# Head pairs of q, k and all of v in products of 512 weight columns, a pad in the pooling pool, and phasors as an outer product

## The chip, the cores and the metric

The kernel runs on one core of a Trainium2 chip. The metric is the device time of one execution in microseconds (us), taken as the median of repeated runs. The profile and the trace are of one execution, recorded by the hardware profiler; that execution has a time of its own, beside the span that the trace covers. The engines are PE (TensorE, matrix products; PEld is its loading of the stationary operand), DVE (VectorE), ACT (ScalarE), POOL (GpSimd), and SP (SyncE), which here only issues DMAs.

## The reference

One block of an encoder: a normalised input of 1024 tokens by 1024 channels is multiplied by a wide weight matrix, the columns go to four mixers, and the gated mixers' outputs are merged.

```python
hn = rms_norm(x, norm_scale[i])
z = hn @ w_in[i]                       # 1024 x 1024 by 1024 x 9216
a_x, a_g, q, k, v, b_g, c_x, c_g, d_x, d_g, merge = jnp.split(z, split_points, axis=-1)
y_a = rglru_mixer(a_x, ...) * jax.nn.silu(a_g)                  # gated linear recurrence
y_b = neighbourhood_attention(q, k, v, ...) * jax.nn.silu(b_g)  # 8 heads of 64 channels
y_c = s5_mixer(c_x, ...) * jax.nn.silu(c_g)                     # diagonal complex recurrence
y_d = pool_mixer(d_x, ...) * jax.nn.silu(d_g)                   # windows of 2, 4, 8, 16
ys = jnp.stack([y_a, y_b, y_c, y_d], axis=2)
gates = jax.nn.sigmoid(merge.reshape(bsz, s, 4, 1024))
merged = jnp.sum(jnp.einsum('bsnw,nwd->bsnd', ys, w_branch[i]) * gates, axis=2)
x = x + merged @ w_out[i]
x = x + jax.nn.sigmoid(x @ ple_gate[i]) * (p[i] @ ple_proj[i])
```

q, k and v are 512 channels each, columns 1024 to 2560 of `w_in`. In the s5 mixer every one of 32 groups has 64 states and two directions, which makes 128 complex decay factors per group; the kernel works on blocks of 8 tokens and needs the powers of a phasor per state for 128 block positions.

## The kernel before

**Products.** Every fp32 operand is split into a high and a low part (`split`, L85: ACT copies the high part, DVE subtracts), and a product is three matmuls (`mm3`, L89): high by high (L94), low by high (L95 in a row of the trace) and high by low (L96). A row names the moving operand, then the stationary one: `ps_z<-wh,hnH` streams weight columns past stationary normalised tokens, `ps_z<-hnH,wh` streams tokens past stationary weights.

**q, k, v.** These are wanted with tokens on the partitions, so the stationary operand is a block of 128 tokens of `hnH` or `hnL` and 256 weight columns move past it (`tok_gen`, L210: 8 token blocks x 8 blocks of the sum x 3 matmuls). `at_z(rd)` (L453) makes 128 columns of q and 128 of k, which is one head pair, for round `rd` of 4; `at_w` (L447) loads them. v is made in two such products (`tok_product`, L418). So six products of 192 matmuls each, of 128x256.

**Fill.** All other columns of z run through `z_gen` (L158): 128 weight columns stationary, 512 tokens moving, 24 matmuls a piece. The generator `fill` (L355) yields these pieces in the order s5 input, gates of branch 2, merge gates 1, and so on; the attention takes one piece of `side` or `fill` for each of its units (`attention`, L400), and the stages s5, glu and lru take as many as `drive` (L189) gives them, to keep PE at work beside DVE. What is left runs before `pool`.

**Buffers.** Raw weights `wr`, their parts `wh` and `wl` (three of each), and two buffers `gz` of 128x1024, used by results that go to DRAM (`su`, `gz`), are shared by all of this. `s5_u` (L892) sends the s5 input to DRAM as `ud` from `gz` buffers, four stores in all. The stages' own buffers come from pools that are opened one after the other in the same memory: `pool` (L697) opens its own (`up`, `pa`, `pm`, ...) where those of `lru` lay, and the merge's (`mp`) are opened ahead of it.

**s5.** `s5_params` (L755) makes tables once. Each of four batches (`s5_batch`, L916) makes its phasors `E` from line 998 on by seven doublings: in each the part done is multiplied by a power `Pm[m]`, on 8, 16, ... 512 elements a partition.

**Order.** The order of the instructions on each engine is set when the kernel is built: a scheduler plays them against a model of the engines, and every engine then runs its list in order. The text of the program, the costs that pieces yield and the pools' buffers decide it together.

Of the kernel before, what the change touches and what calls it, by code (L numbers as in the profile page):

```python
# [9 lines left out]
F32 = mybir.dt.float32  # L10
# [10 lines left out]
W = 512  # L21
# [10 lines left out]
class Kern:  # L32
    def __init__(self, tc, es, ins, out):
# [15 lines left out]
        self.yd = [self.dp.tile([W, S], F32, name=f"yd{n}") for n in range(4)]  # L49

# [149 lines left out]

    def w_tok_halves(self, raw):

        out = []
        for kh in range(2):
            H, L = self.whl([128, 4, 256])
            self.split(H, L, raw[:, 4 * kh:4 * kh + 4, :])
            out += [(H[:, k, :], L[:, k, :]) for k in range(4)]
        return out

    def tok_gen(self, aH, aL, raw, consume):  # L210

        hl = self.w_tok_halves(raw)
        for t in range(8):
            ps = self.ps("z")[:, :256]
            c = slice(t * 128, t * 128 + 128)
            self.mm3(ps, [(aH[k][:, c], aL[k][:, c], hl[k][0], hl[k][1]) for k in range(8)])
            consume(t, ps)
            yield 2.6, 0.0

    def tok_product(self, aH, aL, raw, consume):  # L220
        for _ in self.tok_gen(aH, aL, raw, consume):
            pass
# [151 lines left out]
    def start(self):  # L374
        with self.tc.tile_pool(name="st", bufs=1, reuse_waits="tile") as st:
# [12 lines left out]
            raw0 = self.at_w(0)  # L388
# [5 lines left out]
            self.zq0 = next(self.z0)  # L394
# [5 lines left out]
    def attention(self, ap, fill):  # L400
        nc = self.nc
        vd = self.dp.tile([S, W], F32, name="vd")
        z = [self.at_z(rd) if rd else self.z0 for rd in range(4)]
        zq = [self.zq0]
# [4 lines left out]
        for _ in z[0]:  # L409
            pass  # L410
        prep = self.at_prep(ap, 0, zq[0])
# [3 lines left out]
        for vb in range(2):  # L415
            raw = self.wload_in(2048 + 256 * vb)

            def put_v(t, ps, vb=vb):  # L418
                v = ap.tile([128, 256], F32, tag="vtok", name="vtok", bufs=2)
                self.copy_a(v, ps)  # L420
                nc.sync.dma_start(vd[t * 128:t * 128 + 128, vb * 256:vb * 256 + 256], v)
            self.tok_product(self.hnH, self.hnL, raw, put_v)
            if vb == 0:
                self.lru_consts()
        zq.append(next(z[1]))
        for _ in z[1]:
            pass
        for rd in range(4):
            nxt, prep = None, iter(())
            if rd < 3:  # L430
                prep = self.at_prep(ap, rd + 1, zq[rd + 1])
                nxt = next(prep)
                next(prep)
            side = fill
            if rd < 2:
                side = z[rd + 2]
                zq.append(next(side))
            for u, _ in enumerate(self.at_units(ap, rd, qk, bias, vd)):
                next(side, None)
                if u == 3:  # L440
                    next(prep, None)
            if rd < 2:
                for _ in side:
                    pass
            qk = nxt

    def at_w(self, rd):  # L447
        win = self.i["w_in"]
        return self.wload([(lambda r_, s=s: r_[:, :, s * 128:s * 128 + 128],
                            win[:, c0:c0 + 128].rearrange("(k p) n -> p k n", p=128))  # L450
                           for s, c0 in ((0, 1024 + 128 * rd), (1, 1536 + 128 * rd))])

    def at_z(self, rd, raw=None):  # L453

        raw = raw or self.at_w(rd)
        zqk = self.zp.tile([128, 8, 256], F32, tag="zqk", name="zqk", bufs=2)
        ss = self.zp.tile([128, 32], F32, tag="ss", name="ss", bufs=2)
        yield zqk, ss

        def put(t, ps):  # L460
            self.copy_a(zqk[:, t, :], ps)
# [956 lines left out]
```

## Time and profile before

| | us |
|---|---|
| median of 3 runs | 1363.79 (1362.86 to 1364.15) |
| the profiled execution, its own time | 1363.28 |
| its span in the trace | 1361.5 |
| PE busy | 1346.4 (99%) |
| PEld busy | 1142.4 (84%) |
| DVE busy | 918.7 (67%) |
| ACT busy | 565.0 (41%) |

A busy share says how long at least one instruction of the engine was in work. PE's matmuls overlap, so the duration of one (its latency) is longer than the distance from its start to the next one's start; how many fit into a stretch is read from the distances. A wait is listed with the engine whose result ended it.

### The profile page before, as it was taken

Reading aid. Unit: us, or ns where it says so; the run is one execution under the profiler, and the core shown is the slowest. Engines: PE = TensorE matmul, PEld = TensorE weight load, DVE = VectorE, ACT = ScalarE, POOL = GpSimd, SP = SyncE. Lnnn points to the kernel's source line nnn. Section 1 sums busy time; section 2 is a strip of 40 time slices with the busy share of each in tenths; the row PEclk is TensorE's granted clock in tenths of the full one; section 3 lists DMA queues with packets and bytes.
Section 4 is the critical chain, followed back from the end, with each engine's and each line's share of the span. In section 5 each row is a group of like instructions: output and inputs, shape, how many; then the busy total and the mean of one; then the engine's idle time right before and its main releaser. Section 6 shows DMA issues by size and latency. Waiting matters only on the chain.

```text
span 1361.5 us, 19175 instructions
## 1 busy us (share of the span) xinstructions
PE 1346.4 (99%) x7360; PEld 1142.4 (84%) x7360; DVE 918.7 (67%) x1666; ACT 565.0 (41%) x882; POOL 20.6 (2%) x81
## 2 busy tenths in 40 slices
PE   7999999999999999999999999999999999999998
PEld 6999998888888888788888888888888888888887
DVE  6551676455279797988758477266456667797797
ACT  6542676587532222222225545536321211145553
POOL 2200000000000000000000000000000000000000
PEclk9999999999999999999999999999999999999999
DMA  9452134433244233333344242241834747533435
GB/s 327 130 144 68 51 85 123 132 97 121 85 116 124 81 100 107 110 97 94 128 131 179 70 143 77 97 147 71 298 127 151 248 158 251 212 109 118 130 124 186
DMA packets 141198, 181.98 MB, mean 134 GB/s; under 512 B 29216, under 2 KB 101160, under 8 KB 141106
## 3 DMA queue, kind: packets, MB, share of 16 engines
q1 hardware_dynamic: 140754, 180.72, 40.9%
q8 instruction: 58, 0.95, 0.3%
q14 instruction: 34, 0.28, 0.1%
q0 software_dynamic: 352, 0.03, 0.0%
HBM read 127.05 MB, written 54.03 MB: 133 GB/s over the span
## 4 chain that ended last, share of the span: by engine, by line
PE 92%; DVE 5%; issue 1%; ACT 1%; DMA 0%; SPq 0%; DVEq 0%
PE ps_z L94 15%; PE ps_z L95 15%; PE ps_z L96 15%; PE ps_t L95 4%; PE ps_t L96 4%; PE ps_t L94 4%; PE ps_t L99 3%; PE ps_o L94 3%; PE ps_z L1335 3%; PE ps_t L1335 3%; PE ps_s L1335 3%; PE ps_o L96 3%; PE ps_o L95 3%; PE ps_o L1335 3%; PE ps_s L94 3%; PE ps_s L96 3%
## 5 line engine op out<-in xcount | busy, mean ns | idle before, releaser
L94 PE MATMUL ps_z<-hnH,wh 128*128 128x512 f32 x744 | 293.2, 394 | 2.0 <-DVE bgt L60 2.0
L95 PE MATMUL ps_z<-hnL,wh 128*128 128x512 f32 x744 | 292.0, 392 | 0.0
L96 PE MATMUL ps_z<-hnH,wl 128*128 128x512 f32 x744 | 291.8, 392 | 0.0
L94 PEld LDWEIGHTS ps_z<-hnH,wh 128*128 128x128 f32 x744 | 139.8, 188 | 30.9 <-DVE bgt L60 2.4
L96 PEld LDWEIGHTS ps_z<-hnH,wl 128*128 128x128 f32 x744 | 139.8, 188 | 28.4 <-issue 0.4
L95 PEld LDWEIGHTS ps_z<-hnL,wh 128*128 128x128 f32 x744 | 139.8, 188 | 27.9 <-issue 0.4
L66 DVE TENSOR_TENSOR wl<-wr,wh 128x1024 fp32r<-128x1024 f32 x72 | 88.0, 1222 | 100.8 <-ACT wh L82 100.7
L82 ACT ACTIVATE wh<-wr 128x1024 fp32r<-128x1024 f32 x72 | 76.1, 1059 | 147.5 <-PE ps_z L95 81.2
L94 PE MATMUL ps_z<-wh,hnH 128*128 128x256 f32 x384 | 108.3, 285 | 0.5 <-ACT zqk L82 0.5
L96 PE MATMUL ps_z<-wh,hnL 128*128 128x256 f32 x384 | 108.5, 287 | 0.0
L95 PE MATMUL ps_z<-wl,hnH 128*128 128x256 f32 x384 | 108.1, 283 | 0.0
L95 PE MATMUL ps_t<-hnL,wh 128*128 128x512 f32 x216 | 84.2, 390 | 0.0
L94 PE MATMUL ps_t<-hnH,wh 128*128 128x512 f32 x216 | 84.1, 389 | 0.0
L96 PE MATMUL ps_t<-hnH,wl 128*128 128x512 f32 x216 | 84.0, 389 | 0.0
L94 PEld LDWEIGHTS ps_z<-wh,hnH 128*128 128x128 f32 x384 | 73.3, 192 | 1.2 <-ACT zqk L82 1.2
L95 PEld LDWEIGHTS ps_z<-wl,hnH 128*128 128x128 f32 x384 | 73.5, 192 | 0.0
L96 PEld LDWEIGHTS ps_z<-wh,hnL 128*128 128x128 f32 x384 | 72.9, 192 | 0.0
L551 DVE CUSTOM_DVE_ANT_0 sc<-ps_s,bias 128x384 f32<-128x384 f32 x64 | 34.2, 554 | 27.2 <-PE ps_s L545 14.6
L94 PE MATMUL ps_o<-my,wh 128*128 128x512 f32 x128 | 49.9, 390 | 0.4 <-DVE pm L69 0.4
L78 ACT ACTIVATE gz<-ps_z 128x512 f32<-128x512 f32 x45 | 26.6, 592 | 56.9 <-issue 35.1
L94 PE MATMUL ps_s<-my,wh 128*128 128x512 f32 x128 | 49.8, 389 | 0.0
L96 PE MATMUL ps_s<-my,wl 128*128 128x512 f32 x128 | 49.8, 389 | 0.0
(411 smaller groups left out, 2707.2 us busy)
## 6 DMA issues: line engine op xcount, KB each, us to landing
wr<-in_w_in_dram SPq DMA_DIRECT2D x32, 1024.0 KB, 5.2
gd<-gz SPq DMA_DIRECT2D x32, 512.0 KB, 2.8
mgt<-gd SPq DMA_DIRECT2D x32, 512.0 KB, 4.1
sg<-bgt SPq DMA_DIRECT2D x16, 512.0 KB, 3.2
my<-yd SPq DMA_DIRECT2D x16, 512.0 KB, 4.3
mbr<-in_w_branch_dram SPq DMA_DIRECT2D x8, 1024.0 KB, 6.3
bias<-E SPq DMA_DIRECT2D x128, 48.0 KB, 2.0
xt<-in_x_dram SPq DMA_DIRECT2D x8, 512.0 KB, 10.0
```

The source lines that it names most:

```text
L66: self.nc.vector.tensor_tensor(out, a, b, ALU.subtract)
L78: self.nc.scalar.activation(out, a, f, **kw)
L82: return self.nc.scalar.activation(out, a, AF.Copy)
L94: mm(ps, aH, bH, start=(k == 0), stop=False)
L95: mm(ps, aH, bL, start=False, stop=False)
L96: mm(ps, aL, bH, start=False, stop=(k == n - 1))
L99: self.nc.tensor.transpose(ps, src, self.ident[:k, :k])
L551: nc.vector.tensor_tensor_reduce(sc, pss[h], bias[g][h][:, VIDX[j], :], 1.0, -3e38, ALU.add, ALU.max, mx)
L1335: self.nc.tensor.matmul(acc[g][:, n2], a[:, k, c], b[:, k, n2], start=begin and a is aH and b is bH, stop=end and a is aL, skip_group_chec ...
```

## The change

It has three parts.

1. **Wide products.** `at_z(pr)` makes q and k of two head pairs in one product: 256 columns of q and 256 of k, 512 moving columns. `qk_load` loads them in four DMAs, and `qkv_tiles` splits the weights in four chunks, of which three lie in `wh`/`wl` buffers and the fourth in the two `gz` buffers. v is one product of 512 columns. In rounds 0 and 1 of the attention the side work is now the first half of the s5 input (4 pieces), then the second wide product, then `fill`; the other half of the s5 input opens `fill`.
2. **A pad in `pool`.** One tile of 3600 floats a partition is taken and never used, which puts the following buffers of the pool at higher addresses, behind the memory of `lru`.
3. **Phasors.** `s5_params` makes two small tables for all 32 groups, `Ef` with the first 16 powers and `Eh` with every 16th of 128; a batch multiplies them as an outer product, three operations of 128x1024 for each of the real and imaginary parts.

```diff
...
             self.nc.vector.tensor_copy(self.gT, pt[:, 0:8])
             ple = self.ple(st, *ab, *hl)
             next(ple)
-            raw0 = self.at_w(0)
+            raw0 = self.qk_load(0)
             self.rel_bias()
             self.norm(st, 0, x0)
             for _ in ple:
                 pass
             self.z0 = self.at_z(0, raw0)
-            self.zq0 = next(self.z0)
+            self.zq = next(self.z0)
             for _ in range(4):
                 next(self.z0)
             self.norm(st, 1, x1)
     def attention(self, ap, fill):
         nc = self.nc
         vd = self.dp.tile([S, W], F32, name="vd")
-        z = [self.at_z(rd) if rd else self.z0 for rd in range(4)]
-        zq = [self.zq0]
+        zq = self.zq
         bias = [[ap.tile([128, 3, 384], F32, name=f"bias{g}{h}") for h in range(2)] for g in range(2)]
         for b in bias[0] + bias[1]:
             nc.gpsimd.memset(b, NEG)
         self.at_buffers(ap)
-        for _ in z[0]:
+        for _ in self.z0:
             pass
+        raw_v = self.wide_load("w_in", 2048)
         prep = self.at_prep(ap, 0, zq[0])
         qk = next(prep)
         for _ in prep:
             pass
-        for vb in range(2):
-            raw = self.wload_in(2048 + 256 * vb)
-
-            def put_v(t, ps, vb=vb):
-                v = ap.tile([128, 256], F32, tag="vtok", name="vtok", bufs=2)
-                self.copy_a(v, ps)
-                nc.sync.dma_start(vd[t * 128:t * 128 + 128, vb * 256:vb * 256 + 256], v)
-            self.tok_product(self.hnH, self.hnL, raw, put_v)
-            if vb == 0:
+        for t, ps in self.qkv_tiles(raw_v):
+            v = ap.tile([128, 512], F32, tag="vtok", name="vtok")
+            self.copy_a(v, ps)
+            nc.sync.dma_start(vd[t * 128:t * 128 + 128, :], v)
+            if t == 3:
                 self.lru_consts()
-        zq.append(next(z[1]))
-        for _ in z[1]:
-            pass
+        side = self.z_gen([self.s5_u(0)])
         for rd in range(4):
-            nxt, prep = None, iter(())
-            if rd < 3:
+            prep = iter(())
+            if rd != 1 and rd < 3:
                 prep = self.at_prep(ap, rd + 1, zq[rd + 1])
                 nxt = next(prep)
                 next(prep)
-            side = fill
-            if rd < 2:
-                side = z[rd + 2]
-                zq.append(next(side))
             for u, _ in enumerate(self.at_units(ap, rd, qk, bias, vd)):
                 next(side, None)
+                if rd == 0 and u == 1:
+                    raw1 = self.qk_load(1)
                 if u == 3:
                     next(prep, None)
-            if rd < 2:
-                for _ in side:
-                    pass
+                    if rd == 0:
+                        side = self.at_z(1, raw1)
+                        zq = zq + next(side)
+                    if rd == 1:
+                        side = fill
+                        prep = self.at_prep(ap, 2, zq[2])
+                        nxt = next(prep)
+                if rd == 1 and u in (3, 4):
+                    next(prep, None)
             qk = nxt
 
...
+    def qk_load(self, pr):
+
+        out = []
+        for kh in range(2):
+            r = self.wp.tile([128, 4, 512], F32, tag="wr", name="wr")
+            for s in range(2):
+                c0 = 1024 + 512 * s + 256 * pr
+                self.nc.sync.dma_start(r[:, :, s * 256:s * 256 + 256],
+                                       self.i["w_in"][kh * 512:kh * 512 + 512, c0:c0 + 256]
+                                       .rearrange("(k p) n -> p k n", p=128))
+            out.append(r)
+        return out
+
+    def qkv_tiles(self, raws):
+
+        hl = []
+        for q in range(4):
+            if q < 3:
+                H, L = self.whl([128, 2, 512])
+            else:
+                H, L = (self.gzp.tile([128, 2, 512], F32R, tag="gz", name="w" + c) for c in "hl")
+            self.split(H, L, raws[q // 2][:, q % 2 * 2:q % 2 * 2 + 2, :])
+            hl += [(H[:, k, :], L[:, k, :]) for k in range(2)]
+        for t in range(8):
+            ps = self.ps("z")
+            c = slice(t * 128, t * 128 + 128)
+            self.mm3(ps, [(self.hnH[k][:, c], self.hnL[k][:, c]) + hl[k] for k in range(8)])
+            yield t, ps
+
+    def at_z(self, pr, raws):
+
+        out = [(self.zp.tile([128, 8, 256], F32, tag="zqk", name="zqk", bufs=2),
+                self.zp.tile([128, 32], F32, tag="ss", name="ss", bufs=2)) for _ in range(2)]
+        yield out
+        for t, ps in self.qkv_tiles(raws):
+            for r, (zqk, ss) in enumerate(out):
+                self.copy_a(zqk[:, t, :].rearrange("p (s n) -> p s n", s=2),
+                            ps.rearrange("p (s r n) -> p r s n", s=2, r=2)[:, r])
+                sq = self.zp.tile([128, 4, 64], F32, tag="sq", name="sq", bufs=2)
+                self.act(sq, zqk[:, t, :].rearrange("p (h c) -> p h c", c=64), AF.Square)
+                self.nc.vector.tensor_reduce(ss[:, t * 4:t * 4 + 4], sq, AX.X, ALU.add)
+            yield 5.2, 0.0
 
...
     def pool(self, pp):
         nc, i = self.nc, self.i
         ef = pp.tile([128, 4, 16], F32, name="ef")
+        pp.tile([128, 3600], F32, name="pad")
...
             self.cmul(sp, Pr[:, m + 1, :], Pi[:, m + 1, :], Pr[:, m, :], Pi[:, m, :], Pr[:, m, :], Pi[:, m, :],
                       [128, G])
 
+        self.Ef = [kp.tile([128, G, 16], F32, name=f"Ef{k}") for k in range(2)]
+        self.Eh = [kp.tile([128, G, 8], F32, name=f"Eh{k}") for k in range(2)]
+        for tab, m0, nm in ((self.Ef, 0, 4), (self.Eh, 4, 3)):
+            nc.vector.memset(tab[0][:, :, 0:1], 1.0)
+            nc.vector.memset(tab[1][:, :, 0:1], 0.0)
+            for m in range(nm):
+                n = 1 << m
+                lo, hi = slice(0, n), slice(n, 2 * n)
+                P = [q[:, m0 + m, :].unsqueeze(2).broadcast_to([128, G, n]) for q in self.Pm]
+                for k in range(2):
+                    t = sp.tile([128, G, 8], F32, tag="et", name="et")[:, :, 0:n]
+                    self.mul(tab[k][:, :, hi], tab[k][:, :, lo], P[0])
+                    self.mul(t, tab[1 - k][:, :, lo], P[1])
+                    self.tt(tab[k][:, :, hi], tab[k][:, :, hi], t, ALU.add if k else ALU.subtract)
+
...
         yield 5.0, 1.0
 
         E = [sb.tile([128, 8, 128], F32, tag=f"Gf{k}", name=f"E{k}") for k in range(2)]
-        nc.vector.memset(E[0][:, :, 0:1], 1.0)
-        nc.vector.memset(E[1][:, :, 0:1], 0.0)
-        for m in range(7):
-            n = 1 << m
-            b = [128, 8, n]
-            P = [self.Pm[k][:, m, g8].unsqueeze(2).broadcast_to(b) for k in range(2)]
-            t0 = sb.tile([128, 8, 64], F32, tag="Et", name="Et")[:, :, 0:n]
-            lo, hi = slice(0, n), slice(n, 2 * n)
-            self.mul(E[0][:, :, hi], E[0][:, :, lo], P[0])
-            self.mul(t0, E[1][:, :, lo], P[1])
-            self.sub(E[0][:, :, hi], E[0][:, :, hi], t0)
-            t1 = sb.tile([128, 8, 64], F32, tag="Et", name="Et")[:, :, 0:n]
-            self.mul(E[1][:, :, hi], E[0][:, :, lo], P[1])
-            self.mul(t1, E[1][:, :, lo], P[0])
-            self.add(E[1][:, :, hi], E[1][:, :, hi], t1)
-            yield 0.0, 1.5
+        ev = [128, 8, 8, 16]
+        Hv, Fv = ([t[k][:, g8, :].unsqueeze(ax).broadcast_to(ev) for k in range(2)]
+                  for t, ax in ((self.Eh, 3), (self.Ef, 2)))
+        for k in range(2):
+            o = E[k].rearrange("p g (a b) -> p g a b", b=16)
+            et = sb.tile(ev, F32, tag="tmpA", name="Et")
+            self.mul(o, Hv[0], Fv[k])
+            self.mul(et, Hv[1], Fv[1 - k])
+            self.tt(o, o, et, ALU.add if k else ALU.subtract)
+            yield 0.0, 3.7
...
             return [slice(0, 256), slice(256, 512)]
         return [slice(0, 512)]
 
+    def wide_load(self, n, c0):
+
+        out = []
+        for kh in range(2):
+            r = self.wp.tile([128, 4, 512], F32, tag="wr", name="wr")
+            self.nc.sync.dma_start(r, self.i[n][kh * 512:kh * 512 + 512, c0:c0 + 512]
+                                   .rearrange("(k p) n -> p k n", p=128))
+            out.append(r)
+        return out
+
...
     def run(self):
         tc = self.tc
         with tc.tile_pool(name="gzp", bufs=2, reuse_waits="tile") as self.gzp:
-            fill = self.z_gen([self.s5_u(), self.branch_gate(2, 3584), self.gates(1), self.branch_gate(0, 512), self.branch_gate(3, 4608), self.branch_gate(1, 2560), self.gates(3), self.gates(2), self.gates(0)])
+            fill = self.z_gen([self.s5_u(1), self.branch_gate(2, 3584), self.gates(1), self.branch_gate(0, 512), self.branch_gate(3, 4608), self.branch_gate(1, 2560), self.gates(3), self.gates(2), self.gates(0)])
             with tc.tile_pool(name="zp", bufs=1, reuse_waits="tile") as self.zp:
                 self.start()
                 with tc.tile_pool(name="at", bufs=1, reuse_waits="tile") as ap:
```

The code numbers lines of the changed kernel one higher in the helpers, and about eight higher further down; `L95` of the change is `L94` of before.

PE at the start of the first q and k product, where the token blocks' transposes (`ps_t<-ident,xt`) end; before:

```order
L99 MATMUL ps_t<-ident,xt 128x128 x8
L94 MATMUL ps_z<-wh,hnH 128x256
L95 MATMUL ps_z<-wl,hnH 128x256
L96 MATMUL ps_z<-wh,hnL 128x256
L94 MATMUL ps_z<-wh,hnH 128x256
L95 MATMUL ps_z<-wl,hnH 128x256
L96 MATMUL ps_z<-wh,hnL 128x256
```

and changed:

```order
L100 MATMUL ps_t<-ident,xt 128x128 x4
L95 MATMUL ps_z<-wh,hnH 128x512
L96 MATMUL ps_z<-wl,hnH 128x512
L97 MATMUL ps_z<-wh,hnL 128x512
L95 MATMUL ps_z<-wh,hnH 128x512
L96 MATMUL ps_z<-wl,hnH 128x512
L97 MATMUL ps_z<-wh,hnL 128x512
```

The same three matmuls a block of the sum, on twice as many moving columns; over the whole program 1152 matmuls of 128x256 have become 576 of 128x512.

SP where the s5 input goes to DRAM during the attention (`bias<-E` builds the score tables of the next round in tile number 694 to 697, `vb<-vd` fetches v); before:

```order
L144 DMA wr<-in_w_in_dram 128x8x256
L533 DMA bias_665<-E 16x3x256 x8
L533 DMA bias_666<-E 16x3x256 x8
L902 DMA ud<-su 128x1024
L144 DMA wr<-in_w_in_dram 128x8x256
L902 DMA ud<-su 128x1024
L533 DMA bias_667<-E 16x3x256 x8
L533 DMA bias_668<-E 16x3x256 x8
L902 DMA ud<-su 128x1024
L144 DMA wr<-in_w_in_dram 128x8x256
```

and changed:

```order
L916 DMA ud<-su 128x1024
L145 DMA wr<-in_w_in_dram 128x8x256
L532 DMA bias_694<-E 16x3x256 x8
L532 DMA bias_695<-E 16x3x256 x8
L916 DMA ud<-su 128x1024
L145 DMA wr<-in_w_in_dram 128x8x256
L532 DMA bias_696<-E 16x3x256 x8
L532 DMA bias_697<-E 16x3x256 x8
L519 DMA vb<-vd 32x4x128 x2
L571 DMA yd_75<-yb 128x1024
L519 DMA vb<-vd 32x4x128 x14
```

The first two stores `ud` now stand ahead of and behind sixteen loads of score tables in the first round, and the second wide product, whose fourth chunk takes the two buffers that these stores read, comes after them.

DVE between the end of the recurrence (`ls<-ls,sgl`) and the first pooled tile (`pm<-pa,pup`); before:

```order
L60 TENSOR_TENSOR ls<-ls,sgl 128x1024
L66 TENSOR_TENSOR wl<-wr,wh 128x1024
L66 TENSOR_TENSOR pwL<-pw,pwH 128x128
L60 TENSOR_TENSOR my<-my,myg 128x1024
L66 TENSOR_TENSOR my<-my 128x1024
L60 TENSOR_TENSOR my<-my,myg 128x1024
L66 TENSOR_TENSOR wl<-wr,wh 128x1024
L66 TENSOR_TENSOR my<-my 128x1024
L60 TENSOR_TENSOR my<-my,myg 128x1024
L66 TENSOR_TENSOR my<-my 128x1024
L60 TENSOR_TENSOR my<-my,myg 128x1024
L66 TENSOR_TENSOR wl<-wr,wh 128x1024
```

and changed:

```order
L61 TENSOR_TENSOR ls<-ls,sgl 128x1024
L67 TENSOR_TENSOR wl<-wr,wh 128x1024
L67 TENSOR_TENSOR pwL<-pw,pwH 128x128
L67 TENSOR_TENSOR wl<-wr,wh 128x1024
L61 TENSOR_TENSOR my<-my,myg 128x1024
L64 TENSOR_TENSOR pa<-pup 128x1039
L61 TENSOR_TENSOR my<-my,myg 128x1024
L67 TENSOR_TENSOR my<-my 128x1024
L61 TENSOR_TENSOR pa<-pa,ef 128x1 x2
L67 TENSOR_TENSOR my<-my 128x1024
L70 SCALAR_TENSOR_TENSOR pm<-pa,pup 128x1024
L61 TENSOR_TENSOR my<-my,myg 128x1024
```

The pooling of the first tile moved up between the multiplications by the attention's gate (`my<-my,myg`); on PE, 164 matmuls now lie between the last one of the recurrence and the first one of the pooling, where there were 264.

## Rows read from the trace of the kernel before

**Rows 1.** The profile's page: busy time by engine, shares of the last chain.

```profile
PE 1346.4 (99%) x7360; PEld 1142.4 (84%) x7360; DVE 918.7 (67%) x1666; ACT 565.0 (41%) x882; POOL 20.6 (2%) x81
...
PE 92%; DVE 5%; issue 1%; ACT 1%; DMA 0%; SPq 0%; DVEq 0%
```

**Rows 2.** PE's waits by tile and releaser: total us, times, longest us.

```profile
PE ps_t L99 <- POOL ident masks.py:199: 2.6, 1, 2.6
PE ps_t L99 <- DMA p_tok<-in_p_dram: 2.4, 1, 2.4
PE ps_z L94 <- DVE bgt L60: 2.0, 2, 1.7
PE ps_z L94 <- ACT wh L82: 1.2, 1, 1.2
PE ps_z L94 <- ACT pp_g L82: 0.7, 1, 0.7
PE ps_z L94 <- ACT zqk L82: 0.5, 2, 0.4
```

**Rows 3.** Windows: stretch, length, busy PE, PEld, DVE, ACT, POOL, clock, DMA.

```profile
0.00:25.00 25.00, 18.04 (x70) 13.91 (x71) 13.65 (x30) 14.22 (x23) 4.13 (x11) 1.00 0.92 336
100.00:125.00 25.00, 25.00 (x209) 25.00 (x208) 4.44 (x8) 7.04 (x16) 0.00 (x0) 1.00 0.38 110
900.00:925.00 25.00, 25.00 (x112) 20.69 (x111) 7.17 (x7) 6.61 (x9) 0.00 (x0) 1.00 0.48 168
```

**Rows 4.** The page's groups, matmuls of 256 and 512 columns: busy, mean ns.

```profile
L94 PE MATMUL ps_z<-wh,hnH 128*128 128x256 f32 x384 | 108.3, 285 | 0.5 <-ACT zqk L82 0.5
...
L94 PE MATMUL ps_t<-hnH,wh 128*128 128x512 f32 x216 | 84.1, 389 | 0.0
```

**Rows 5.** Timeline of PE in a product of v: start us, duration us.

```profile
99.78 0.28 PE L96 MATMUL ps_z<-wh,hnL 128*128 128x256 f32 x1
...
101.58 0.28 PE L96 MATMUL ps_z<-wh,hnL 128*128 128x256 f32 x1
```

**Rows 6.** Timeline of PE in the fill pieces.

```profile
909.83 0.39 PE L96 MATMUL ps_t<-hnH,wl 128*128 128x512 f32 x1
...
912.55 0.39 PE L96 MATMUL ps_t<-hnH,wl 128*128 128x512 f32 x1
```

**Rows 7.** DVE by line, whole span: the phasors' multiplications of all sizes.

```profile
L60 DVE TENSOR_TENSOR Et<-E,Pm 128x8 f32<-128x8 f32 (+6 forms) x56 | 17.4, 310 | 1.4
...
L60 DVE TENSOR_TENSOR E<-E,Pm 128x8 f32<-128x8 f32 (+6 forms) x56 | 15.2, 304 | 0.0
```

**Rows 8.** DVE by shape, 500 to 700 us: xcount, busy us, mean ns.

```profile
L60 DVE TENSOR_TENSOR E<-E,Pm 128x256 f32<-128x256 f32 x6 | 2.3, 419 | 0.0
...
L60 DVE TENSOR_TENSOR E<-E,Pm 128x32 f32<-128x32 f32 x6 | 0.9, 184 | 0.0
```

**Rows 9.** Timeline of SP: score table issues behind an s5 input store.

```profile
240.80 0.33 SPq L902 DMA_DIRECT2D ud<-su  x1
241.67 8.07 SPq L533 DMA_DIRECT2D bias<-E  x16
```

**Rows 10.** Timeline of PE: the recurrence's last matmul, the pooling's first.

```profile
934.40 0.39 PE L96 MATMUL ps_o<-xH,gL 128*128 128x512 f32 x1
...
994.25 0.62 PE L94 MATMUL ps_o<-pmH,pwH 128*128 128x512 f32 x2
```

**Rows 11.** Timeline of DVE between these two: gated rows, first pooled tile.

```profile
961.34 1.23 DVE L60 TENSOR_TENSOR my<-my,myg 128x1024 f32<-128x1024 f32 x1 [5.43 <-DMA myg<-sg]
...
965.08 1.22 DVE L60 TENSOR_TENSOR my<-my,myg 128x1024 f32<-128x1024 f32 x1 [0.16 <-DMA pw<-in_pool_w_dram]
...
987.34 1.22 DVE L69 SCALAR_TENSOR_TENSOR pm<-pa,pup 128x1024 f32<-128x1024 f32 x1
```

**Rows 12.** Timeline of ACT: pooled channels from PSUM, high part of pm.

```profile
984.54 0.58 ACT L82 ACTIVATE pup<-ps_t 128x512 f32<-128x512 f32 x1
988.60 1.06 ACT L82 ACTIVATE pmH<-pm 128x1024 fp32r<-128x1024 f32 x1 [3.48 <-DVE pm L69]
```

More of the change, by code (lines that the diff above doesn't have):

```diff
@@ L49, in __init__ @@
         self.yd = [self.dp.tile([W, S], F32, name=f"yd{n}") for n in range(4)]
+        self.ud = self.dp.tile([W, 8, 128], F32, name="ud")
     def ps(self, tag):
@@ L199, in drive @@
                     pe, dve = pe + c[0], dve + c[1]
[L201 to L221, printed above, removed]
-            pass
     def consts(self):
@@ L433, in attention @@
                 next(prep)
-            side = fill
-            if rd < 2:
-                side = z[rd + 2]
-                zq.append(next(side))
             for u, _ in enumerate(self.at_units(ap, rd, qk, bias, vd)):
                 next(side, None)
+                if rd == 0 and u == 1:
+                    raw1 = self.qk_load(1)
                 if u == 3:
                     next(prep, None)
-            if rd < 2:
-                for _ in side:
-                    pass
-            qk = nxt
@@ L447, in at_w @@
[L447 to L461, printed above, removed]
-            sq = self.zp.tile([128, 4, 64], F32, tag="sq", name="sq", bufs=2)
-            self.act(sq, zqk[:, t, :].rearrange("p (h c) -> p h c", c=64), AF.Square)
-            self.nc.vector.tensor_reduce(ss[:, t * 4:t * 4 + 4], sq, AX.X, ALU.add)
-        yield from self.tok_gen(self.hnH, self.hnL, raw, put)
+                    if rd == 0:
+                        side = self.at_z(1, raw1)
+                        zq = zq + next(side)
@@ L890, in s5_params, with s5_u @@
             nc.vector.tensor_copy(self.I16[p, :], self.ident[p, p])
-    def s5_u(self):
-        self.ud = self.dp.tile([W, 8, 128], F32, name="ud")
+    def s5_u(self, blk):
         us = {}
@@ L901, in put @@
             if hf == 1:
-                self.nc.sync.dma_start(self.ud[ct * 128:ct * 128 + 128], us[0])
-        return 3072, 2, put
+                self.nc.sync.dma_start(self.ud[(2 * blk + ct) * 128:(2 * blk + ct) * 128 + 128], us[0])
+        return 3072 + 256 * blk, 1, put
     def s5(self):
```

## The prediction

> **What bounds the kernel now.** I began with the busy time by engine and the shares of the chain that ended last [rows 1]: PE is busy for 1346.4 of 1361.5 us and holds 92% of the chain. What the change can give is therefore time that PE works, or time that it waits. The list of PE's waits [rows 2] says how little the second is: 2.6 and 2.4 us stand at the very start, before any product can run, and of the rest the largest are 2.0 us for `bgt` in the s5 stage, 1.2 for the first weights, 0.7 and 0.5. The window of the first 25 us [rows 3] shows the start: PE works 18.04 of them with the DMA engines 92% busy. In windows further on PE works 25.00 of 25 at a granted clock of 1.00, the 2.4 GHz level [rows 3]. So I read what a matmul costs where PE is full.
>
> Here two views say different things. In the groups [rows 4] a matmul of 256 columns lasts 285 ns and one of 512 columns 389 ns. These are latencies; neighbours overlap. The distances are in the timelines: in a product of v sixteen starts lie between 99.78 and 101.58, which is 1.80 / 15 = 120.0 ns each [rows 5]; in the fill thirteen starts lie between 909.83 and 912.55, 2.72 / 12 = 226.7 ns [rows 6]. The windows agree: 209 matmuls of 256 columns in 25 us, 119.6 ns, and 112 of 512, 223 ns [rows 3]. The 256 columns more cost 106.7 ns, so 13.3 ns belong to each matmul whatever its width.
>
> **The change part by part.**
>
> *Wide products.* 1152 matmuls of 256 columns become 576 of 512. By the timelines that is 1152 x 120.0 = 138.2 us against 576 x 226.7 = 130.6 us, **7.7 us less** on the path (576 x 13.3 ns). From the windows' counts it would be 576 x (2 x 119.6 - 223) = 9.3 us; a window counts one matmul at each edge that is only partly in it, so 223 is low, and I take 7.7. Loading stationary operands is no new limit: PEld is busy for 25.00 us of the window of 256 columns, but for 20.69 in that of 512, with a load for every matmul in both [rows 3]. Splitting the weights, copying the results and the DMAs move the same bytes, in the same or fewer instructions, on engines with 59% and 33% of the span free [rows 1].
>
> A rule speaks against this. The Trainium skill, "TensorE: Matmul & The Clock Gate", section "Wait — 56ns, not 53.3ns?", gives a warm matmul its columns at 2.4 GHz and about 2.5 ns. By it the doubling would save 2.5 ns a pair, 1.4 us in all by its estimate, and the sum would end near 1362. The trace disagrees: its distance of 120.0 ns is 13.3 ns over the columns, not 2.5 [rows 5].
>
> *Buffers of the wide products.* Four chunks of weights need four pairs of buffers, and the fourth is the two `gz`. At the first two products nothing else uses these. In round 0 it is otherwise: the fourth chunk of the second wide product waits until both `ud` stores have read their buffers, and the second store stands on SP behind sixteen issues of score tables, which took 8.07 us in such a place [rows 9]. The split of that chunk on DVE stands ahead of softmax work. PE needs it after 18 matmuls of the first token block, 18 x 226.7 ns = 4.1 us into the product, and has attention units ahead of it. Counting those, I find the split done some 3 us before. Bounds: 0 and, if the whole row of issues falls late, 5 us; I take 0.5.
>
> *The attention's other waits.* The 0.5 us for `zqk` [rows 2] are waits for copies of a 256-column product, where a token block lasts 24 x 120.0 ns = 2.9 us; in the change it lasts 24 x 226.7 ns = 5.4 us, with two copies, so PE waits less. I take 0.5 us off. The start loads 1 MB more for the first product while the DMA engines are 92% busy [rows 3], but PE then has 5.4 us of work for each token block ready: bounds -1 and +3 us, taken 0.
>
> *Phasors.* The 112 multiplications take 17.4 + 15.2 = 32.6 us [rows 7], 291 ns each; the 56 additions and subtractions on the same sizes, which I put at the same mean, make it 49 us in all. Instead there are 24 operations of 128x1024, at 1.22 us as the pooling's [rows 11] 29 us, and 42 small ones once, at 184 to 419 ns [rows 8], 8 to 18 us; of these only 6 have the largest size and 24 the two smallest, so I take 11. DVE gains 9 us. PE waits for DVE in this stage for 2.0 us in two places [rows 2], both because a multiplication by `bgt` came late behind the batch's scans. The tables add some 11 us of DVE work in a row at the stage's start, where PE also wants `bgt`; a new wait of 1 to 2 us is likely there, and the others may go. Bounds -2 and +3, taken 0.
>
> *Pool.* Four fill pieces have moved into the attention, so 164 matmuls, 164 x 226.7 ns = 37.2 us, lie between the recurrence's last matmul and the first of the pooling, where there were 59.9 us [rows 10]. The chain that PE meets there was ready early: the second half of `pup` was copied at 984.54, `pm` ran at 987.34, and `pmH` was done at 988.60 + 1.06 = 989.66 [rows 11, 12], 4.6 us before its use at 994.25 [rows 10]. In the change the copies of `pup` come 100 x 226.7 ns = 22.7 us earlier relative to the recurrence, the second 984.54 + 0.58 - 934.40 - 22.7 = 28.0 us behind it; the gated rows do not, as they wait for DMAs behind the recurrence's end. Their multiplications ran at 961.34 and 965.08, which is 26.9 and 30.7 us after 934.40 [rows 10, 11]. The new order on DVE has `pa` after the first and `pm` behind the second and the two subtractions of these: 30.7 + 1.22 + 2 x 1.23 + 0.25 + 1.22 = 35.9 us, and 1.06 us on ACT make 36.9, against PE's need at 37.2. That is just in time, and the following tiles are as tight. Without the pad the chain would wait longer still, for the recurrence's buffers. Bounds 0 and 13 us, taken 1.
>
> **The sum** against the profiled execution: 1363.3 - 7.7 + 0.5 - 0.5 + 0 + 1 = 1356.6 us. PE's smaller waits elsewhere, `wh` and `pp_g` with 1.9 us together [rows 2], lie at the start, where the wider product gives PE more to do; I take 1 us off: **1355.6**. The median stands 0.5 us over the profiled execution, so 1356.
>
> **The rivals.**
>
> *All waits shrink.* PE's waits of 2.0 + 1.2 + 0.7 + 0.5 = 4.4 us [rows 2] go, and none comes: 1363.8 - 7.7 - 4.4 = 1351.7. For it: DVE gets freer. Against it: the tight chain at the pooling. 0.12, between 1350 and 1353.
>
> *New waits eat most of the gain.* The store of `ud` is late by 5 us, or tables and pooled tiles cost as much together: 1356 + 5 = 1361. For it: PE has no slack, so each late buffer shows. Against it: the count leaves some 3 us. 0.10, between 1359 and 1363.
>
> *The wide matmul keeps no fixed time to save.* Stationary blocks of tokens with a moving weight of 512 columns don't stand in the trace; if such a matmul took close to 2 x 120.0 ns, nearly nothing would be saved, and the time would lie between 1362 and 1364. Against it: the fill changes its stationary operand at every matmul too and runs at 226.7 [rows 6]. 0.05. The Trainium skill's rule named above would end in the same place.
>
> *Slower: the pooled tiles come late.* Place: PE between the recurrence and the merge. DVE stands at a multiplication `my<-my,myg` until that row has landed, with the pooling behind it. In the trace it sat idle 5.43 us at the first of them [rows 11]. If the second lands 13 us later, for instance because the gated rows queue behind a weight load that SP now issues ahead of them, PE waits about 12.5 us there: 1356 + 12.5 = 1368.5. It decides from a wait of 10.5 us on (7.7 saved and 2.7 more); below it the kernel is still not slower. For it: a margin of 0.3 us. Against it: the rows' loads don't depend on the moved pieces. 0.07.
>
> *The latencies taken as costs:* 576 x (2 x 285 - 389) = 104 us less, 1260 [rows 4]. The distances speak against it. 0.01.
>
> **How the numbers follow.** The forecast, 1354 to 1358.5, has 0.65. Within 1350 and 1362 lie it, the first rival and most of the second, together about 0.85. A change of 0.2%, 2.7 us, is about what a measurement can tell from none, so faster means below 1361.1: 0.65 + 0.12 + 0.05 + 0.01 = 0.83; the same: the other half of the second rival and the third, 0.10; slower 0.07.
>
> **What would show it.** In the trace of the changed kernel: products of 512 columns of weights at distances of 227 ns, with PE's busy time down by about 7.7 us and its waits about as long as before. A wait of `ps_z` for `wl` or `gz` in the attention would be the `ud` store; one of `ps_o` for `pmH` or `pmL`, the pooling; DVE's phasor lines should fall by 9 us net of the tables' without PE showing it. Wrong would be a distance above 235 ns, or waits of more than 8 us that are not in the list of before.

## The result, and the profile after

The changed kernel takes 1373.69 us (median of 6 runs, 1369.73 to 1375.88) against 1363.51 of the kernel before: a ratio of 1.0071, 95% interval 1.0051 to 1.0091 (ratios here are of the runs' means). It is 0.7% slower, where 1356 was forecast with a range of 1350 to 1362. The profiled execution took 1375.87 us, with a span of 1373.9 where the span before was 1361.5.

The busy times and the shares of the chain, against [rows 1]:

```profile
PE 1348.8 (98%) x6784; PEld 1114.4 (81%) x6784; DVE 912.3 (66%) x1560; ACT 575.6 (42%) x884; POOL 20.8 (2%) x81
...
PE 90%; DVE 6%; DMA 1%; ACT 1%; issue 1%; SPq 0%; DVEq 0%; ACTq 0%
```

PE has 576 instructions less and is busy 2.4 us more: something took more time than the products gave back. The first place to look is PE's list of waits (columns as in [rows 2]):

```profile
PE ps_z L95 <- ACT wh L83: 6.0, 4, 2.2
PE ps_s L95 <- ACT ygH L84: 2.6, 1, 2.6
PE ps_t L100 <- POOL ident masks.py:199: 2.6, 1, 2.6
PE ps_t L100 <- DMA p_tok<-in_p_dram: 2.3, 1, 2.3
PE ps_z L95 <- DVE bgt L61: 2.1, 2, 1.5
PE ps_z L95 <- DVE xs L1058: 1.1, 1, 1.1
PE ps_z L97 <- DVE wl L67: 1.0, 1, 1.0
```

Three lines behind s5 are new or have grown against [rows 2]: `wh`, 6.0 us in four places where it was 1.2 in one at the start, `ygH` with 2.6 (the glu stage's operand), and `wl` with 1.0. None of them is at a place that the prediction spoke of. A fourth, `xs` with 1.1, lies in s5. Windows of PE around these waits (columns as in [rows 3]) add a second loss:

```profile
740.00:750.00 10.00, 10.00 (x45) 8.08 (x44) 8.22 (x9) 7.85 (x11) 0.00 (x0) 1.00 0.70 279
750.00:760.00 10.00, 7.37 (x24) 5.43 (x24) 5.32 (x6) 4.42 (x6) 0.27 (x4) 0.83 0.01 2
...
770.00:780.00 10.00, 7.32 (x22) 5.28 (x21) 7.22 (x8) 2.21 (x3) 0.26 (x1) 0.74 0.54 178
780.00:790.00 10.00, 9.08 (x37) 7.12 (x36) 1.10 (x2) 2.62 (x4) 0.53 (x1) 0.92 0.22 68
...
820.00:830.00 10.00, 7.81 (x26) 5.61 (x26) 8.70 (x9) 7.34 (x10) 0.53 (x1) 0.83 0.39 130
```

In a full window PE starts 45 matmuls in 10 us at a granted clock of 1.00; here it starts 22 to 37, and the clock is 0.74 to 0.92. The timeline of PE at the recurrence's first products (start us, duration us) shows both losses, the wait and the clock after it:

```profile
773.41 0.50 PE L95 MATMUL ps_z<-hnH,wh 128*128 128x512 f32 x1 [1.70 <-ACT wh L83]
...
775.59 0.80 PE L97 MATMUL ps_z<-hnH,wl 128*128 128x512 f32 x1 [0.98 <-DVE wl L67]
776.18 0.63 PE L95 MATMUL ps_z<-hnH,wh 128*128 128x512 f32 x1
776.61 0.63 PE L96 MATMUL ps_z<-hnL,wh 128*128 128x512 f32 x1
777.04 0.63 PE L97 MATMUL ps_z<-hnH,wl 128*128 128x512 f32 x1
```

Behind the waits the starts lie 0.43 us apart, 512 columns at the 1.2 GHz level, until 781.3.

To see where the 12.4 us between the two spans come from, I took the distance between neighbouring starts on PE, less the median distance of that form in undisturbed runs, and summed what remains over the span:

| | before | changed |
|---|---|---|
| sum of the median distances (the work) | 1327.4 | 1319.9 |
| excess over 0.15 us each behind 25 us (gaps and the refill behind them) | 6.1 | 18.6 |
| 512-column matmuls at the lower clock | 0.0 | 5.4 |
| excess under 0.15 us each | 12.8 | 15.0 |
| excess in the first 25 us | 7.7 | 7.5 |

The work shrank by 7.5 us, the gaps grew by 12.5, the lower clock took 5.4 and the small excesses 2.2. The run to run spread (1369.73 to 1375.88) goes with the clock: the runs near 1370 have a mean of 0.998, those near 1375 one of 0.994 to 0.995.

### The profile page after: what moved, and what is told of

Read it like the earlier page. It is cut to its first block, busy times and chain, and to the rows that moved or that the text cites. A ratio compares the mean times of both kernels' runs of the same rounds, so it can differ in the third digit from the quotient of the medians.

```text
span 1373.9 us, 17902 instructions
## 1 busy us (share of the span) xinstructions
PE 1348.8 (98%) x6784; PEld 1114.4 (81%) x6784; DVE 912.3 (66%) x1560; ACT 575.6 (42%) x884; POOL 20.8 (2%) x81
## 4 chain that ended last, share of the span: by engine, by line
PE 90%; DVE 6%; DMA 1%; ACT 1%; issue 1%; SPq 0%; DVEq 0%; ACTq 0%
PE ps_z L95 15%; PE ps_z L97 15%; PE ps_z L96 15%; PE ps_t L100 3%; PE ps_t L96 3%; PE ps_t L95 3%; PE ps_t L97 3%; PE ps_z L1353 3%; PE ps_t L1353 3%; PE ps_s L1353 3%; PE ps_o L1353 3%; PE ps_o L95 3%; PE ps_o L97 3%; PE ps_o L96 3%; PE ps_s L96 2%; PE ps_s L97 2%
## 5 line engine op out<-in xcount | busy, mean ns | idle before, releaser
L95 PE MATMUL ps_z<-hnH,wh 128*128 128x512 f32 x760 | 301.7, 397 | 7.9 <-ACT wh L83 4.8
L97 PE MATMUL ps_z<-hnH,wl 128*128 128x512 f32 x760 | 301.0, 396 | 1.0 <-DVE wl L67 1.0
L96 PE MATMUL ps_z<-hnL,wh 128*128 128x512 f32 x760 | 299.9, 395 | 0.0
L95 PEld LDWEIGHTS ps_z<-hnH,wh 128*128 128x128 f32 x760 | 144.0, 189 | 39.1 <-ACT wh L83 6.0
L96 PE MATMUL ps_t<-hnL,wh 128*128 128x512 f32 x200 | 78.0, 390 | 0.0
L95 PE MATMUL ps_t<-hnH,wh 128*128 128x512 f32 x200 | 77.9, 390 | 0.0
L95 PE MATMUL ps_z<-wh,hnH 128*128 128x512 f32 x192 | 75.6, 395 | 0.5 <-ACT zqk L83 0.5
L96 PE MATMUL ps_z<-wl,hnH 128*128 128x512 f32 x192 | 75.1, 393 | 0.0
L97 PE MATMUL ps_z<-wh,hnL 128*128 128x512 f32 x192 | 74.7, 396 | 0.0
L95 PE MATMUL ps_o<-my,wh 128*128 128x512 f32 x128 | 49.9, 390 | 0.4 <-DVE pm L70 0.4
L97 PE MATMUL ps_o<-my,wl 128*128 128x512 f32 x128 | 49.8, 389 | 0.0
L96 PE MATMUL ps_o<-my,wh 128*128 128x512 f32 x128 | 49.8, 389 | 0.0
L95 PE MATMUL ps_s<-my,wh 128*128 128x512 f32 x128 | 49.8, 389 | 0.0
L96 PE MATMUL ps_s<-my,wh 128*128 128x512 f32 x128 | 49.8, 389 | 0.0
```

The costliest lines, as they stand in the source:

```text
L95: mm(ps, aH, bH, start=(k == 0), stop=False)
L96: mm(ps, aH, bL, start=False, stop=False)
L97: mm(ps, aL, bH, start=False, stop=(k == n - 1))
```

## What the waits have in common

The gaps lie where s5 ends and `glu` and `lru` begin. There PE waits for parts of weights and for a chain on DVE and ACT, which the fill should cover. I counted, in the program, how many half pieces of fill (24 matmuls, 24 x 226.7 ns = 5.4 us, one call of the generator; the text ahead of the result calls these 24 a piece) each stage takes. Two half pieces share one pair of weight parts `wh`, `wl`, of which there are three buffers; the next piece's pair is made one piece ahead.

| half pieces | attention | s5 and the calls behind it | glu | recurrence and after | time, us |
|---|---|---|---|---|---|
| before | 16 | 50 | 8 | 30 | 1363.5 |
| changed | 24 | 47 | 8 | 25 | 1373.7 |

`drive` (L189) deals half pieces against the costs that a stage yields. In a batch of s5 the phasors yielded seven times 1.5, 10.5; now they yield twice 3.7, 7.4. Four batches yield 12.4 less, and s5 takes three half pieces less, 16 us of PE's work. The attention takes eight more. So later stages have five less, PE comes to glu with less cover behind it, and 47 is odd: at the start of glu and of the recurrence the fill stands in the middle of a piece. That half-used piece holds one weight buffer, the prepared next one a second, and the recurrence's own first products, which stand ahead of both in the list, have one buffer left. Each of their weights can then be split only when PE has finished with what lay there before.

That is **theory A**: the odd number holds the buffers (waits for `wh`, `wl`), and the missing cover uncovers the chain to `ygH`. Rivals: **B**, the eight half pieces more that the attention takes leave too few for the later stages; **C**, the phasors' operations in their new order on DVE delay s5. **D** is for the third part: without the pad the pooled channels' buffers wait for the recurrence.

## The experiments

The kernel before ran beside each set, at 1363.2, 1363.2 and 1363.4 us.
With an odd number in the second column glu begins in the middle of a piece of fill.

| run | half pieces in s5 and the calls | at glu | us | ratio to before, 95% |
|---|---|---|---|---|
| third_piece | 48 | between pieces | 1358.71 | 0.9965 [0.9952, 0.9978] |
| before_one_less | 49 | in a piece | 1378.90 | 1.0113 [1.0097, 1.0129] |
| old_costs | 50 | between | 1368.83 | 1.0042 [1.0027, 1.0057] |
| wide_only | 50 | between | 1367.76 | 1.0030 [1.0019, 1.0040] |
| one_call | 46 | between | 1371.38 | 1.0057 [1.0042, 1.0072] |
| wide_pad | 50 | between | 1366.33 | 1.0025 [1.0015, 1.0035] |
| third_no_pad | 48 | between | 1359.36 | 0.9970 [0.9958, 0.9982] |
| phasors_third | 48 | between | 1376.85 | 1.0100 [1.0085, 1.0115] |
| old_costs_no_call | 48 | between | 1358.46 | 0.9965 [0.9952, 0.9978] |
| wide_pad_no_call | 48 | between | 1357.76 | 0.9959 [0.9944, 0.9974] |
| phasors_old_costs | 50 | between | 1367.82 | 1.0033 [1.0022, 1.0045] |
| pad_only | 50 | between | 1363.22 | 0.9998 [0.9989, 1.0008] |

The runs that start from the kernel before (before_one_less, phasors_third, phasors_old_costs, pad_only) have 16 half pieces in the attention, all others 24.

**third_piece: one half piece more in the changed kernel.**

```diff
             next(fill)
             next(fill)
+            next(fill)
```

> The changed kernel, with one more half piece of fill taken between the s5 and the glu stage (three calls in place of two), nothing else. In the changed kernel the s5 stage takes 45 half pieces and the two calls 2, an odd number, so that glu and the recurrence begin in the middle of a fill piece, whose weights then hold one of the three buffers while the next piece's prepared weights hold a second. Theory A (the half piece at the stage's start): 48 half pieces, both stages begin between pieces, the waits for wh, wl and ygH between 745 and 830 us go with the stretches at the lower clock: 1355 to 1358 us. Theory B (four fill pieces too few are left for glu and the recurrence, since the attention uses them up): one more is taken earlier, so the waits stay or grow: 1370 us or more. Theory C (the phasors' new order on DVE delays the stage): unchanged, 1370 to 1376.

1358.71 us, just above the 1355 to 1358 expected under theory A. One half piece, work that is done either way, is worth 15 us. PE's waits:

```profile
PE ps_t L100 <- DMA p_tok<-in_p_dram: 2.6, 1, 2.6
PE ps_t L100 <- POOL ident masks.py:199: 2.6, 1, 2.6
PE ps_z L95 <- DVE bgt L61: 2.1, 2, 1.5
PE ps_z L95 <- DVE xs L1058: 1.1, 1, 1.1
PE ps_z L95 <- ACT wh L83: 0.9, 1, 0.9
```

`ygH` and `wl` are gone, and what is left of `wh` lies in the first 25 us; no matmul behind 25 us runs at the lower clock. B and C fall as causes of the loss: the attention still takes its eight more, and the phasors are the new ones.

**before_one_less: the kernel before with an odd number.**

```diff
             next(fill)
-            next(fill)
```

> The kernel before, with one call in place of two between the s5 and the glu stage, nothing else: 49 half pieces in place of 50, so that both later stages begin in the middle of a fill piece, with the old products, the old phasors and no pad. Theory A: the waits of the changed kernel appear here, 1363.5 + 10 to 17 = 1373 to 1380 us. Theory B: one half piece more is left for the later stages, so no loss: 1363 to 1364. Theory C: nothing of the phasors is changed: 1363 to 1364.

1378.90 us: the kernel before, with none of the change's parts, lost 15.7 us by one call. Its waits are those of the changed kernel:

```profile
PE ps_z L94 <- ACT wh L82: 5.9, 4, 2.2
PE ps_s L94 <- ACT ygH L83: 2.8, 1, 2.8
...
PE ps_z L96 <- DVE wl L66: 2.0, 1, 2.0
```

They lie in the same two stages, between 716 and 797 us here, and 22 matmuls of 512 columns behind them ran at the lower clock. That the missing half piece makes the loss as a whole is shown, in the old and in the new kernel. Which of theory A's two parts, the middle of a piece or the missing cover, makes which wait, these two runs don't tell, as both change together.

**one_call: an even number, but smaller.**

```diff
             next(fill)
-            next(fill)
```

(in the changed kernel)

> The changed kernel with one call of the fill between s5 and glu in place of two: 46 half pieces, so that glu and the recurrence begin between pieces, as with three calls, but with two half pieces less done by then. Tells the half piece from the mere count. Theory A (the half piece holds a pair of weight buffers): the waits for wh and wl at the recurrence's start go; the wait for ygH, which ends a chain of DVE and ACT that the fill before glu covers, stays at 2 to 8 us: 1358 to 1364. If the count alone decides: more waits than in the changed kernel, 1375 or more.

1371.38 us, above what I expected, but the split between the two waits is as theory A has it:

```profile
PE ps_s L95 <- ACT ygH L84: 6.6, 1, 6.6
...
PE ps_s L95 <- DVE m L61: 1.4, 1, 1.4
...
PE ps_z L95 <- ACT wh L83: 1.1, 1, 1.1
```

Between pieces the waits for `wh` at the recurrence go (1.1 us is the start's). `ygH` counts the cover alone: 6.6 us with 46 half pieces, 2.6 with 47, none with 48, steps of up to 4 us where a half piece is 5.4. By the account used above, one_call has 9.6 us more of gaps and refills than third_piece and 1.4 more at the lower clock. That is of the profiled execution, the fastest of four (1369.83); why the median lies 1.5 us higher, no trace shows.

The programs as built show the buffers. In the changed kernel the half-used piece keeps one `wh` buffer through glu, the prepared piece a second, and the first two weight parts of the recurrence both lie in the third, where glu's last weights lay. So ACT splits the first only behind glu's last matmul, which starts at 771.33, and the second only when PE has used up the first:

```profile
772.31 1.05 ACT L83 ACTIVATE wh<-wr 128x1024 fp32r<-128x1024 f32 x1
...
788.50 1.06 ACT L83 ACTIVATE wh<-wr 128x1024 fp32r<-128x1024 f32 x1 [3.64 <-PE ps_t L96]
```

In third_piece the two lie in different buffers and are split at 766.56 and 771.75; PE comes to the first at 771.07. The third wait, 2.2 us at 824.86, is not for a buffer: the last matmul on that buffer starts at 814.34, but ACT has the split in its list behind the recurrence's activations and comes to it at 823.75.

**old_costs and wide_only: an even number that is larger.**

```diff
-            yield 0.0, 3.7
+            yield 0.0, 5.25
```

> The changed kernel, with the two costs that a batch's phasors yield to the planner raised from 3.7 to 5.25 each, so that their sum is 10.5 as before the change; the operations are the same. The s5 stage then takes 48 half pieces, and glu begins between pieces. Theory A: 1355 to 1358 us. Theory B: two to three half pieces more are used up before glu, so the waits stay or grow: 1370 or more. Theory C: 1370 to 1376.

wide_only leaves the pad and the phasors' part of the change out:

```diff
-        pp.tile([128, 3600], F32, name="pad")
...
```

> The kernel before with the wide products of q, k and v and what they bring with them (order of side work in the attention, the s5 input in two halves), without the pad and with the old phasors and their old costs. The fill then stands between pieces at glu and at the recurrence. Theory A: 1363.5 - 7.7 = 1356 us, up to 1358 if the pooling waits. Theory B: the four pieces used up in the attention are missing later: 1370 or more. Theory C: 1356.

1368.83 and 1367.76: theory A's numbers were wrong here. glu and the recurrence start clean, but the waits have gone to the pooling and to the merge's products beside it (`m`). old_costs:

```profile
PE ps_s L95 <- DVE m L61: 4.6, 1, 4.6
...
PE ps_z L95 <- ACT pup L83: 1.4, 1, 1.4
...
PE ps_o L95 <- ACT pmH L83: 0.7, 1, 0.7
```

and wide_only:

```profile
PE ps_z L95 <- ACT pup L83: 7.1, 1, 7.1
```

Here theory B holds in part. Of 104 half pieces 24 go to the attention and 8 to glu; with 50 before glu, 22 are left for the recurrence, all of them used up by its end, and PE comes to the pooling some 11 us early (my estimate, two half pieces of 5.4). With 48 there are 24 and no such wait. In the kernel before, 30 were left.

**wide_pad, third_no_pad, pad_only: the pad.** The pad added to wide_only; taken from third_piece; added to the kernel before.

> The kernel before with the wide products and the pad, with the old phasors and costs; against the run with the wide products alone (1367.8, of which 7.1 us were a wait for the copy of pup) it differs in the pad alone. Theory D (without the pad the pooled channels' buffers wait for the recurrence's last work on the same memory): the wait for pup shrinks below 2 us, 1360 to 1363; what stays are waits in the pooling, as the glu stage has used up two half pieces more than with three calls. If the pad does nothing: 1368.

> The changed kernel with three calls between s5 and glu (1358.7) and without the pad. Theory D: a wait for pup of 5 to 7 us at the pooling's start, 1363 to 1366. If the pad does nothing here: 1358 to 1359.

> The kernel before with the pad alone. Where six half pieces of fill and the gated rows lie between the recurrence and the pooling, the pooled channels' buffers are free early anyway: 1363 to 1364, no change. If the pad moved other buffers into a conflict: above 1366.

With 22 left for the recurrence the pad takes the wait for `pup` from 7.1 to 1.4 us, as theory D has it, but the next waits take its place, and of the 5 us that I expected 1.4 remain (1367.76 to 1366.33, with intervals that overlap). wide_pad:

```profile
PE ps_s L95 <- DVE m L61: 4.0, 1, 4.0
...
PE ps_z L95 <- ACT pup L83: 1.4, 1, 1.4
...
PE ps_o L95 <- ACT pmH L83: 0.7, 1, 0.7
```

With 24, and in the kernel before, it does nothing that can be told: 1359.36 without against 1358.71 with, 1363.22 against 1363.41. The 5 to 7 us that I expected of third_no_pad were wrong.

**phasors_third, phasors_old_costs: the phasors alone.** Both are the kernel before with the new tables and operations; the first with the new costs and three calls, the second with the old costs and two.

> The kernel before with the new phasors alone, and three calls between s5 and glu, so that both stages begin between pieces. What the phasors give by themselves. By the prediction's step: DVE is busy for 9 us less, PE's waits in s5 stay at about 2 to 4 us: 1362 to 1365. If the new order on DVE costs PE more: above 1366.

> The kernel before with the new phasors at the old costs (5.25 twice), two calls: 50 half pieces, dealt out as before. The phasors' operations by themselves. If only the costs did the harm in the run with the phasors alone (1376.9, a wait for ygH of 7.5 us): 1361 to 1364. If the operations or their order on DVE delay the chain: a wait for ygH of 2 us or more stays, 1366 or more.

1376.85 and 1367.82. In the first, with 48 half pieces where the old kernel has 50, PE waits 7.5 us for `ygH` in two places. That fits the missing cover: the programs made from the kernel before wait 0, 2.8 and 7.5 us for `ygH` with 50, 49 and 48, those made from the changed one 0, 2.6 and 6.6 with 48, 47 and 46. Why the changed program does with two fewer, no run shows. So this run doesn't price the phasors. In the second the number is the old one; no wait for `ygH` is left, which was the sign that I had expected with such a time, and 4.4 us are still lost. Its waits in s5:

```profile
PE ps_s L1077 <- DMA M<-kd: 1.8, 1, 1.8
PE ps_z L94 <- DVE bgt L60: 1.5, 1, 1.5
...
PE ps_z L94 <- DVE xs L1059: 1.1, 1, 1.1
...
PE ps_s L1077 <- DVE xs L1060: 0.6, 1, 0.6
PE ps_s L1079 <- DVE Xr L66: 0.5, 1, 0.5
```

With 0.2 us more for `bgt` these are 5.7 us, against 2.0 before; 1.8 of them are for a DMA. Gaps and refills sum to 10.8 us against 6.1 before. So, in the old surroundings, theory C has a part of its own: the new phasors make DVE's work shorter, and PE's gaps in s5 4 to 5 us longer. Why the scattered small operations suit PE better than six large ones, I did not settle.

**old_costs_no_call, wide_pad_no_call: 48 again, and the phasors on and off.** Both have no call between s5 and glu, so that `drive` deals out all 48; they differ in the phasors' operations.

> The changed kernel with the phasors' old costs (5.25 twice) and no call of the fill between s5 and glu: 48 half pieces, as with three calls, but all of them dealt out inside s5. If the number of half pieces done before glu decides (theory A with the count): 1357 to 1360, no waits for ygH or for wh and wl at the recurrence's start. If the costs themselves (where in s5 the fill lies) decide: waits of 3 us or more in s5 or glu, 1362 or more.

> The wide products and the pad with the old phasors, and no call between s5 and glu: 48 half pieces in s5. Against old_costs_no_call it differs in the phasors' operations alone. If the new phasors shorten the chain to ygH by part of DVE's 9 us: a wait for ygH of 3 to 6 us here, 1361 to 1365. If they are worth nothing on the path: 1357 to 1360.

1358.46 with the new phasors, 1357.76 with the old ones: no difference that can be told. With 50 half pieces and two calls the same pair is old_costs and wide_pad, 2.5 us apart with intervals that overlap. Against old_costs and wide_pad only the two calls differ: 50 half pieces cost 10.4 and 8.6 us more than 48. That old_costs_no_call and third_piece agree (1358.46, 1358.71), with the same number dealt out in other places, says that the number decides, not the places. wide_pad_no_call has the lowest median of the study, 0.9959 [0.9944, 0.9974] of before. Its waits:

```profile
PE ps_z L95 <- DVE xs L1049: 1.7, 1, 1.7
PE ps_z L95 <- ACT wh L83: 1.3, 1, 1.3
PE ps_z L95 <- DVE bgt L61: 1.2, 1, 1.2
...
PE ps_s L96 <- DVE ygL L70: 0.5, 1, 0.5
```

By the account used above, it has 7.5 us less work than the kernel before and 1.2 us more gaps; its span is 6.1 us shorter.

## Why the prediction was wrong

- **The products' term was right.** It was put at 7.7 us, and the sum of the median distances fell by 7.5. In the changed kernel's first wide product:

```profile
59.75 0.39 PE L96 MATMUL ps_z<-wl,hnH 128*128 128x512 f32 x1
...
61.34 0.39 PE L97 MATMUL ps_z<-wh,hnL 128*128 128x512 f32 x1
```

  Seven distances in 1.59 us, 227 ns each, with the weights moving, as in [rows 6]. The Trainium skill's rule ("TensorE: Matmul & The Clock Gate", section "Wait — 56ns, not 53.3ns?") would have given 1.4 us, by an estimate from it; the trace disagrees, and its 7.5 us decide.
- **The step that failed is *Phasors*, "Bounds -2 and +3, taken 0".** It priced the operations that the change takes away and adds, and read PE's waits for them. It did not price the third thing that the edit changes: the costs yielded to `drive`, 10.5 to 7.4 a batch. Those moved three half pieces, 16 us of PE's work, from ahead of glu to behind it, and let glu and the recurrence begin in the middle of a piece. One half piece put back gives 15.0 us (third_piece), five times the upper bound. All three put back by the old costs give only 4.9 (old_costs, 1368.83), as the later stages then run short. So the old costs alone would not have saved the forecast: what it lacked is the count of fill by stage, here and in *Pool*.
- DVE's own time was sized well, and gained nothing. The phasors take 24 operations of 128x1024 and 42 small ones; the large ones in the changed kernel's DVE groups:

```profile
L58 DVE TENSOR_TENSOR E<-E,Et 128x1024 f32<-128x1024 f32 x8 | 9.8, 1224 | 0.2
L61 DVE TENSOR_TENSOR Et<-Eh,Ef 128x1024 f32<-128x1024 f32 x8 | 9.8, 1223 | 0.2
...
L61 DVE TENSOR_TENSOR E<-Eh,Ef 128x1024 f32<-128x1024 f32 x8 | 9.7, 1218 | 0.0
```

  29.3 us, with 11 us of small ones, against 50 before: 9 us less, as predicted. DVE's busy time, which counts overlapping operations once, fell by 5.7 from the phasors alone (913.0 in phasors_old_costs against 918.7). In the old surroundings, with the old number of half pieces, the kernel was slower by 4.4 us for it; in the changed ones, with 48, nothing could be told.
- ***Pool* had the right result, in part by luck.** It said that four of its pieces (half pieces here) had moved into the attention and found the chain just in time; in the changed kernel PE waits there for 0.4 us, as the kernel before waited for the same `pm` at the same step. By the count the attention takes eight more and s5 gives three back. It did not see that the number left for the recurrence and the pooling depends on what s5 takes: with 22 left in place of 24 or 25 (old_costs, wide_only) PE waits about 7 us there.
- ***Buffers of the wide products*, the `ud` stores: taken 0.5, measured none.** No wait of the changed kernel names `gz` or `wl` in the attention. The 0.5 us off for `zqk` and the 1 us off at the start did not come either: `zqk` is again 0.5, and the excess in the first 25 us is 7.5 where it was 7.7.
- **The rivals.** *New waits eat most of the gain* came nearest, but it named other places, and its 5 us were too few. *Slower* named the pooling, which is not where it happened. No rival had a changed number of pieces, though the part on the pooling worked with that number. The prediction's own sign of being wrong came true: waits that were not in the list of before sum to 9.5 us (4.8 for `wh` behind the start, 2.6, 1.1 and 1.0), more than its 8.
- **The clock** was in no step. By the table above it cost 5.4 us at 1.2 GHz, and a part of the 2.2 us of small excesses, behind the waits at glu and the recurrence.

## What to carry to other kernels

Where a planner deals filler work against costs that the stages state, such a cost is an instruction: an edit that makes a stage cheaper also takes cover from the next one, and the cover has to be counted in pieces before and after, stage by stage. Count too in which phase the filler is interrupted: a piece in the middle holds its buffers while the next stage wants the same ones. When a change in such a kernel is slower than its parts, shift the filler by half a piece before changing anything else; here one line was worth 15 us, and of the numbers tried in the changed kernel (46, 47, 48 and 50 of 104) only 48 kept the gain.

## What the runs showed of the hardware

PE's granted clock fell behind short waits, to the 1.2 GHz level for 7 to 14 matmuls of 512 columns (0.43 us apart in place of 0.227): 29 in the changed kernel, behind waits of 2.6 and 2.2 us and behind one of 1.0 us that followed 2 us after one of 1.7; 22 in before_one_less. At single waits of 1.5 and 1.1 us in s5 (third_piece) and of 1.7 us (the kernel before) it did not fall. What else decides, these runs don't show.
